# Three Newton steps instead of four in the reciprocal square root of a two-model transformer kernel

## The chip, the cores and the metric

The kernel runs on one core of one Trainium2 chip. The metric is the device time of one execution in microseconds (us), as the median of several runs; lower is better. Before the change three runs gave a median of 2302.99 us (2299.04 to 2307.05). TensorE (PE in the profile, with PEld for its weight loads) multiplies matrices, VectorE (DVE) and ScalarE (ACT) work elementwise, GpSimd (POOL) helps with elementwise work, and SyncE (SP) issues the DMAs.

## The reference, cut to what matters

Two small transformer blocks are computed one after the other on 512 tokens (and 256 context tokens) of width 1024. The first block has a linear recurrence layer (an RWKV-7 mixer with 16 heads, scanned forwards and backwards) and a differential attention layer; the second has two layers that mix causal, dilated and memory attention. The change touches only the normalisations, which stand in nearly every stage:

```python
def rms_norm(x, g, eps=RMS_EPS):
    xf = x.astype(jnp.float32)
    y = xf * lax.rsqrt(jnp.mean(xf * xf, axis=-1, keepdims=True) + eps)
    return (y * g.astype(jnp.float32)).astype(x.dtype)
...
    kk = heads(k * k_k)
    kk = kk * lax.rsqrt(jnp.sum(kk * kk, axis=-1, keepdims=True) + 1e-12)
...
    y = ((o - mean) * lax.rsqrt(var + GN_EPS)).reshape(B, T, RW_WIDTH) * gn_g + gn_b
```

## The kernel before

All large products are written as three TensorE products of a value split in two parts (high and low), so TensorE carries the bulk. The work falls into stages that follow each other in time, here with their place in the trace:

- 0 to 33 us, `startup` (L106): token blocks are loaded, normalised, turned with TensorE and modulated, while 1 MB weight pieces `ada_w` come in.
- 33 to 520 us, the input projections (`project`, L246) of the recurrence layer, with the preparation of the scan (`prep`, `products`, `invert`) woven in. `head_rsqrt` (L260) normalises the keys of each of 8 feature blocks, and of two memory blocks.
- 520 to 1115 us, the recurrence itself (`chain`) and its readouts (`readout`, L898 to L909), then the output projection of that layer.
- 1115 to 1600 us, the differential attention layer (`phase_4`): `Dense.heads` (L1276) makes normalised queries and keys, `attention` uses them. For each head pair, attention of one pair is interleaved with the projections of the next; the first pair's projections (`kqv(0)`) stand alone.
- 1600 to 2300 us, the two layers of the second block (`phase_5`), built alike from `Dense.heads`, `values`, `gates` and `attention`; each begins with a memory query projection (`mem(0)`) and ends with an output projection (`out_layer`), whose `Norm.rstd` (L1446 on) makes the next layer's norm.

The reciprocal square root is a helper, `rsqrt_dve` (L67 to L77). It makes a first guess from the bits of the value (L72) and then improves it in Newton steps of three VectorE instructions each (L74, L75, L76), every one of which reads the result of the one before. The tiles are small, 128 partitions by 1 to 24 numbers. It is called at eight places, 64 times in a run: `startup` L135 (3 times, tile `v`), `head_rsqrt` L272 (10, `hr_v`), `memory_norm` L416 (2, `m_v`), `readout` L899 and L906 (5, `vc`), `Dense.heads` L1300 (22, `hsv`), `Norm.rstd` L1452 (14, `nv`) and the end of a head in `phase_4`, L1607 (8, `ovv`). So L74, L75 and L76 run 256 times each.

The result is used right behind the last step: in `heads` by a multiplication on VectorE (L1303) that TensorE's transposes (L1359) wait for, in `phase_4` by L1608 before the transposes of L1611, in `readout` by a ScalarE copy (L873) before those of L876, in `startup` by L137 before those of L142, in `head_rsqrt` by a ScalarE copy (L274) before those of L280.

Each engine runs its instructions in the order of its own queue. That order is not the order of the Python code: the program is traced in an order that weaving loops set by credits (`weave`, `run_streams`) and priorities, and a planner then lays out each engine's queue by simulating a timeline in which each instruction has a modelled cost:

```python
    with tile.TileContext(nc, schedule_with_timeline_sim=True) as tc:
        run(tc, i, out)
```

So instructions of one Newton chain can stand between those of other work on VectorE's queue. One kind of such work is the weight split (L1071 and L1073): ScalarE rounds a raw weight tile `w_raw` to `w_hi`, and VectorE (90 times) or GpSimd (30 times) subtracts to get `w_lo`, which the projections' matmuls (L1092) read.

Of the kernel before, what the change touches and what calls it, by code (L numbers as in the profile page):

```python
# [66 lines left out]
def rsqrt_dve(E, pool, v, n):  # L67

    nc = E.nc
    y = pool.tile([128, n], FT, name="rq_y", bufs=2)  # L70
    t = pool.tile([128, n], FT, name="rq_t", bufs=2)
    nc.vector.tensor_scalar(y.bitcast(I32), v.bitcast(I32), -0.5, float(0x5F3759DF), OP.mult, OP.add)  # L72
    for _ in range(4):
        nc.vector.tensor_tensor(t, y, y, OP.mult)  # L74
        nc.vector.scalar_tensor_tensor(t, t, -0.5, v, OP.mult, OP.mult)  # L75
        nc.vector.scalar_tensor_tensor(y, t, 1.5, y, OP.add, OP.mult)  # L76
    return y  # L77
# [28 lines left out]
def startup(E, hh, hl):  # L106
# [3 lines left out]
    with tc.tile_pool(name="su", bufs=1, reuse_waits="tile") as pool, \  # L110
# [18 lines left out]
        for b0, nb in ((0, 2), (2, 2), (4, 2)):  # L129
            for tb in range(b0, b0 + nb):  # L130
                junk = pool.tile([128, 1024], FT, name="junk", bufs=1)
                A.activation(junk, xs[:, tb, :], AF.Square, accum_out=ss[:, tb:tb + 1])
            v = pool.tile([128, nb], FT, name="v", bufs=2)
            V.tensor_scalar(v, ss[:, b0:b0 + nb], 1.0 / 1024, 1e-6, OP.mult, OP.add)
            r = rsqrt_dve(E, pool, v, nb)  # L135
            for j in range(nb):
                V.tensor_scalar(xs[:, b0 + j, :], xs[:, b0 + j, :], r[:, j:j + 1], None, OP.mult)  # L137
            for kb in range(0, 8, 2):
                ps = pp.tile([128, 2, nb, 128], FT, name="tp", bufs=2)
                for k in range(2):  # L140
                    for j in range(nb):
                        P.transpose(ps[:, k, j, :], xs[:, b0 + j, (kb + k) * 128:(kb + k + 1) * 128], E.ident)  # L142
                (A.copy if kb % 4 else V.tensor_copy)(
                    xt[:, kb:kb + 2, b0 * 128:(b0 + nb) * 128].rearrange("p k (j t) -> p k j t", j=nb), ps)
# [61 lines left out]
class Scan:  # L206
# [53 lines left out]
    def head_rsqrt(self, x, n, scale, eps, use):  # L260

        E, nc = self.E, self.E.nc
        sq = self.s3("sq")
        nc.scalar.activation(sq[:, :n], x, AF.Square)
        ps = self.px()
        nb = n // 128
        for b in range(nb):
            nc.tensor.matmul(ps[:, 2 * b:2 * b + 2], sq[:, b * 128:(b + 1) * 128], self.ones2, start=True, stop=True)
        v = self.dp.tile([128, 12], FT, name="hr_v", bufs=1)
        nc.vector.tensor_scalar(v[:, :2 * nb], ps[:, :2 * nb], scale, eps, OP.mult, OP.add)  # L270
        yield 0
        r = rsqrt_dve(E, self.dp, v[:, :2 * nb], 2 * nb)  # L272
        rb = sq
        nc.scalar.copy(rb[:, :n].rearrange("p (b d) -> p b d", d=64), r.unsqueeze(2).to_broadcast([128, 2 * nb, 64]))  # L274
        yield 0
        for a in range(0, n, 384):
            m = min(384, n - a)
            ps = self.px()
            for o in range(0, m, 128):
                nc.tensor.transpose(ps[:, o:o + 128], rb[:, a + o:a + o + 128], E.ident)  # L280
            use(ps[:, :m], a, m)
            yield 0
# [123 lines left out]
    def memory_norm(self):  # L406

        E, nc = self.E, self.E.nc
        for b in range(2):
            m, u = (self.dp.tile([128, 8, 128], FT, name="ada_s", bufs=2) for _ in range(2))  # L410
            flat = lambda t: t.rearrange("p k t -> p (k t)")
            nc.sync.dma_start(flat(m), E.i["mem"][b * 128:(b + 1) * 128])
            ss, v = (self.dp.tile([128, 1], FT, name=n, bufs=1) for n in ("m_ss", "m_v"))
            nc.scalar.activation(flat(u), flat(m), AF.Square, accum_out=ss)
            nc.vector.tensor_scalar(v, ss, 1.0 / 1024, 1e-6, OP.mult, OP.add)
            r = rsqrt_dve(E, self.dp, v, 1)  # L416
            nc.vector.tensor_scalar(m, m, r, None, OP.mult)
            yield 0
            for k in (0, 4):
                ps = self.px()  # L420
                for kb in range(4):
                    nc.tensor.transpose(ps[:, kb * 128:(kb + 1) * 128], m[:, k + kb, :], E.ident)
                nc.scalar.copy(flat(u)[:, k * 128:k * 128 + 512], ps)
                yield 0
            nc.sync.dma_start(E.MT[:, :, b * 128:(b + 1) * 128], u)
# [1525 lines left out]
```

## Time and profile before

| what | value |
|---|---|
| median of three runs | 2302.99 us (2299.04 to 2307.05) |
| the profiled execution, its own time | 2302.14 us |
| its span, first to last instruction | 2300.3 us |
| granted TensorE clock, mean over the span | 0.935 |
| PE busy | 2093.5 us, 91% |
| DVE busy | 1574.1 us, 68%, 3952 instructions |
| ACT busy | 1167.7 us, 51% |
| POOL busy | 688.1 us, 30% |

The busy time of an engine is the sum of what its instructions took. A group line gives a source line, the engine, what was written from what, the count, the busy time and the mean length of one, and then the idle time just before these instructions with what ended it. The chain of waits goes back from the last instruction: at each step to what released it, or to the instruction ahead of it on its engine; it is one path, and its pieces are times on that path. A timeline row is a start, a length, the engine and the line, and in brackets the idle time before it.

### The profile page before, as it was taken

Reading aid. Unit: us, or ns where it says so; the run is one execution under the profiler, and the core shown is the slowest. Engines: PE = TensorE matmul, PEld = TensorE weight load, DVE = VectorE, ACT = ScalarE, POOL = GpSimd, SP = SyncE. Lnnn points to the kernel's source line nnn. Section 1 sums busy time; section 2 is a strip of 40 time slices with the busy share of each in tenths; the row PEclk is TensorE's granted clock in tenths of the full one; section 3 lists DMA queues with packets and bytes.
Section 4 is the critical chain, followed back from the end, with each engine's and each line's share of the span. In section 5 each row is a group of like instructions: output and inputs, shape, how many; then the busy total and the mean of one; then the engine's idle time right before and its main releaser. Section 6 shows DMA issues by size and latency. Waiting matters only on the chain.

```text
span 2300.3 us, 49070 instructions
## 1 busy us (share of the span) xinstructions
PE 2093.5 (91%) x18914; PEld 1861.9 (81%) x18920; DVE 1574.1 (68%) x3952; ACT 1167.7 (51%) x2636; POOL 688.1 (30%) x993
## 2 busy tenths in 40 slices
PE   7999999987998988888979999997899999999989
PEld 3998899975777766666979889887888988888878
DVE  5468968987278887734676786854686674767673
ACT  4455456563255453433346465563465564556652
POOL 0133523534036363322312232312222232033221
PEclk9999999985999788877999999998999999999999
DMA  7467456347644333154121111142222223322132
GB/s 248 137 188 235 158 172 220 114 144 230 204 115 139 105 98 115 34 163 159 56 70 49 60 42 65 42 124 79 97 83 68 80 74 108 113 65 65 60 104 81
DMA packets 189592, 262.55 MB, mean 114 GB/s; under 512 B 16048, under 2 KB 136368, under 8 KB 189232
## 3 DMA queue, kind: packets, MB, share of 16 engines
q1 hardware_dynamic: 189360, 259.43, 35.6%
q8 instruction: 149, 2.44, 0.4%
q14 instruction: 83, 0.68, 0.1%
HBM read 196.72 MB, written 62.65 MB: 113 GB/s over the span
## 4 chain that ended last, share of the span: by engine, by line
PE 45%; DVE 13%; DMA 5%; ACT 4%; issue 3%; POOL 2%; SPq 0%; ACTq 0%; DVEq 0%; POOLq 0%
PE ps_pj L1092 25%; PE ps_s L1389 3%; DMA w_raw<-in_wd_dram 2%; PE ps_t L1781 2%; PE ps_t L1599 2%; PE ps_b L579 1%; PE ps_s L1092 1%; PE ps_t L1767 1%; PE ps_m L85 1%; DMA w_raw<-att 1%; DVE hx L1303 1%; DVE w_lo L1073 1%; PE ps_t L1359 1%; PE ps_t L1588 1%; DVE al L556 1%
## 5 line engine op out<-in xcount | busy, mean ns | idle before, releaser
L1092 PE MATMUL ps_pj<-w_hi,act 128*128 128x256 f32 x3264 | 646.3, 292 | 22.0 <-ACT act L1472 4.8
L1092 PEld LDWEIGHTS ps_pj<-w_hi,act 128*128 128x128 f32 x3264 | 530.6, 196 | 36.0 <-ACT act L1472 7.0
L1092 PE MATMUL ps_pj<-w_lo,act 128*128 128x256 f32 x1632 | 472.7, 290 | 0.0
L1092 PEld LDWEIGHTS ps_pj<-w_lo,act 128*128 128x128 f32 x1632 | 320.0, 196 | 1.2 <-issue 0.9
L246 PE MATMUL ps_pj<-h,b_hi 128*128 128x384 f32 (+1 forms) x1216 | 316.4, 341 | 2.7 <-ACT gh L352 1.5
L246 PEld LDWEIGHTS ps_pj<-h,b_hi 128*128 128x128 f32 x1216 | 220.1, 193 | 8.6 <-ACT gh L352 2.7
L246 PE MATMUL ps_pj<-h,b_lo 128*128 128x384 f32 (+1 forms) x608 | 207.3, 342 | 0.4 <-DVE b_lo L190 0.4
L1071 ACT CAST w_hi<-w_raw 128x1024 fp32r<-128x1024 f32 x120 | 121.2, 1050 | 63.0 <-DMA w_raw<-in_wd_dram 33.0
L1073 DVE TENSOR_TENSOR w_lo<-w_raw,w_hi 128x1024 fp32r<-128x1024 f32 x90 | 121.7, 1358 | 40.9 <-ACT w_hi L1071 40.1
L1073 POOL TENSOR_TENSOR w_lo<-w_raw,w_hi 128x1024 fp32r<-128x1024 f32 x30 | 72.5, 2415 | 252.5 <-ACT w_hi L1071 252.5
L1092 PE MATMUL ps_pj<-act,w_hi 128*128 128x256 f32 x768 | 145.7, 285 | 0.0
L1757 POOL TENSOR_SCALAR p<-p,r 128x128 f32<-128x128 f32 (+2 forms) x64 | 71.6, 1119 | 236.5 <-DVE r L1751 151.1
L579 PE MATMUL ps_b<-al,bk 64*128 64x128 f32 x768 | 123.8, 303 | 11.0 <-DVE rbk L587 9.9
L579 PEld LDWEIGHTS ps_b<-al,bk 64*128 64x128 f32 x768 | 102.6, 202 | 32.8 <-issue 20.1
L1092 PEld LDWEIGHTS ps_pj<-act,w_hi 128*128 128x128 f32 x768 | 120.7, 191 | 0.4 <-issue 0.2
L246 PEld LDWEIGHTS ps_pj<-h,b_lo 128*128 128x128 f32 x608 | 117.2, 193 | 3.6 <-issue 1.3
L547 POOL TENSOR_TENSOR s<-bk,src 64x256 f32<-64x256 f32 x96 | 77.5, 807 | 124.0 <-DVE bk L544 111.5
L1092 PE MATMUL ps_pj<-act,w_lo 128*128 128x256 f32 x384 | 109.7, 286 | 0.0
L1315 POOL TENSOR_TENSOR hx<-hx,ctab 128x256 f32<-128x256 f32 x80 | 67.1, 857 | 135.9 <-DVE ht L1313 119.7
L1578 POOL TENSOR_TENSOR p<-p 128x768 f32<-128x768 f32 x32 | 60.6, 1894 | 154.3 <-ACT p L1577 81.5
L1389 PE MATMUL ps_s<-k_s,q_hi 128*128 128x256 f32 (+2 forms) x256 | 88.5, 355 | 9.8 <-ACT p L1748 5.9
L189 ACT CAST b_hi<-b_raw 128x512 fp32r<-128x512 f32 x84 | 52.1, 622 | 71.1 <-PE ps_pj L246 56.6
(325 smaller groups left out, 4943.9 us busy)
## 6 DMA issues: line engine op xcount, KB each, us to landing
w_raw<-in_wd_dram SPq DMA_DIRECT2D x120, 512.0 KB, 4.2
b_raw<-in_blocks_dram SPq DMA_DIRECT2D x84, 256.0 KB, 3.1
src<-streams SPq DMA_DIRECT2D x48, 384.0 KB, 3.8
ada_s<-in_ada_w_dram SPq DMA_DIRECT2D x24, 512.0 KB, 4.4
vs<-streams SPq DMA_DIRECT2D x48, 256.0 KB, 3.2
ada_w<-in_ada_w_dram SPq DMA_DIRECT2D x8, 1024.0 KB, 11.0
lr<-lora SPq DMA_DIRECT2D x96, 64.0 KB, 3.1
streams<-k SPq DMA_DIRECT2D x32, 192.0 KB, 2.8
```

The source lines that it names most:

```text
L189: nc.scalar.copy(hi, raw)
L246: E.nc.tensor.matmul(ps[gi][:, :m], w[:, kb % 4, :], h[:, kb, :], start=(n[gi] == 1), stop=(n[gi] == 24))
L547: G.tensor_tensor(v3(rev(s))[a:a + 64], ut[a:a + 64, 1 if a == 0 else 0], v3(rev(r))[a:a + 64], OP.mult)
L579: P.matmul(pb[:, c, :], bk[q:e, c].rearrange("p s t -> p (s t)"), al[q:e, c, h:3:2 - h, :], start=True, stop=True, tile_position=(q, 0))
L1071: nc.scalar.copy(hi[:, a:a + 4], raw)
L1073: e.tensor_tensor(lo[:, a:a + 4], raw, hi[:, a:a + 4], OP.subtract)
L1092: E.nc.tensor.matmul(ps, a(kb), b(kb), start=(k == 0), stop=(k == 23))
L1315: G.tensor_tensor(w4(x), w4(x), cb, OP.mult)
L1389: P.matmul(ps, q[i][:, 2 * j + h, c], k[h][:, j, a:a + n], start=(i == 0), stop=(stop and i == 1))
L1578: G.tensor_tensor(ps_[0], ps_[0], ps_[1], OP.add)
L1599: P.matmul(ps[:, :128], pt[:, kb, :], v[:, kb, h * 128:(h + 1) * 128], start=(kb == 0), stop=(kb == 5))
L1757: G.tensor_scalar(t, t, r[:, h:h + 1], None, OP.mult)
```

## The change

The loop in `rsqrt_dve` runs three times instead of four; nothing else is edited.

```diff
@@ -70,7 +70,7 @@
     y = pool.tile([128, n], FT, name="rq_y", bufs=2)
     t = pool.tile([128, n], FT, name="rq_t", bufs=2)
     nc.vector.tensor_scalar(y.bitcast(I32), v.bitcast(I32), -0.5, float(0x5F3759DF), OP.mult, OP.add)
-    for _ in range(4):
+    for _ in range(3):
         nc.vector.tensor_tensor(t, y, y, OP.mult)
         nc.vector.scalar_tensor_tensor(t, t, -0.5, v, OP.mult, OP.mult)
         nc.vector.scalar_tensor_tensor(y, t, 1.5, y, OP.add, OP.mult)
```

## Rows read from the trace of the kernel before

**Rows 1.** The page's busy time, share of the span and instructions of each engine.

```profile
PE 2093.5 (91%) x18914; PEld 1861.9 (81%) x18920; DVE 1574.1 (68%) x3952; ACT 1167.7 (51%) x2636; POOL 688.1 (30%) x993
```

**Rows 2.** Busy time in windows: window, length, engines (counts), clock, DMA share, GB/s.

```profile
33.00:520.00 487.00, 473.09 (x3265) 427.51 (x3263) 368.47 (x788) 261.58 (x545) 163.08 (x290) 0.97 0.54 171
660.00:1050.00 390.00, 341.94 (x4883) 272.51 (x4882) 285.48 (x661) 177.61 (x368) 163.90 (x336) 0.86 0.38 112
1180.00:1600.00 420.00, 385.49 (x2979) 365.06 (x2978) 287.78 (x733) 232.88 (x506) 115.95 (x83) 0.96 0.20 64
2000.00:2230.00 230.00, 216.26 (x1749) 196.72 (x1749) 166.24 (x446) 139.80 (x356) 68.04 (x61) 0.99 0.24 75
```

**Rows 3.** VectorE's busy time in L74 to L76 alone, over the whole span.

```profile
0.00:2301.00 2301.00, 172.16 (x768) 0.93 0.36 114
```

**Rows 4.** Timeline of one call at the end of the readouts, last step.

```profile
1053.85 0.17 DVE L76 SCALAR_TENSOR_TENSOR rq_y<-rq_t,rq_y 128x16 f32<-128x16 f32 x1
1054.06 0.17 DVE L74 TENSOR_TENSOR rq_t<-rq_y 128x16 f32<-128x16 f32 x1
1054.26 0.17 DVE L75 SCALAR_TENSOR_TENSOR rq_t<-rq_t,vc 128x16 f32<-128x16 f32 x1
1054.47 0.18 DVE L76 SCALAR_TENSOR_TENSOR rq_y<-rq_t,rq_y 128x16 f32<-128x16 f32 x1
1054.68 1.14 ACT L873 COPY rb<-rq_y 128x512 f32<-128x512 f32 x2 [4.61 <-DVE rq_y L76]
```

**Rows 5.** The chain of waits: first, three long and last piece of L74 to L76.

```profile
1052.17 0.18 DVE rq_t L74
...
1125.06 0.74 DVE rq_y L76
...
1378.19 2.34 DVE rq_y L76
...
2185.30 2.05 DVE rq_t L75
...
2191.39 0.19 DVE rq_y L76
```

**Rows 6.** TensorE's waits: line waited for, us in total, times, longest.

```profile
PE ps_t L1359 <- DVE hx L1309: 11.5, 3, 5.0
...
PE ps_t L1611 <- DVE o L1608: 7.7, 3, 4.3
...
PE ps_m L876 <- ACT rb L873: 3.6, 1, 3.6
...
PE ps_x L280 <- ACT sq L274: 2.5, 1, 2.5
```

**Rows 7.** Timeline of the startup, first call and what follows it.

```profile
15.17 0.16 DVE L76 SCALAR_TENSOR_TENSOR rq_y<-rq_t,rq_y 128x2 f32<-128x2 f32 x1
...
15.39 6.08 PE L85 MATMUL ada_ps<-ada_w,cs 128*2 128x256 f32 x16 [15.39 <-DVE rq_y L76]
...
21.40 1.09 PE L142 MATMUL tp<-ident,x_in 128*128 128x128 f32 x8
```

**Rows 8.** Timeline of a GpSimd weight split beside the end of a call.

```profile
1378.12 2.39 POOL L1073 TENSOR_TENSOR w_lo<-w_raw,w_hi 128x1024 fp32r<-128x1024 f32 x1 [1.17 <-ACT w_hi L1071]
1378.19 2.33 DVE L76 SCALAR_TENSOR_TENSOR rq_y<-rq_t,rq_y 128x4 f32<-128x4 f32 x1
...
1380.56 0.69 DVE L1608 TENSOR_TENSOR o<-o,rq_y 128x512 f32<-128x512 f32 x1
```

**Rows 9.** Timeline of the first call in the attention layer.

```profile
1178.96 0.18 DVE L72 TENSOR_SCALAR rq_y<-hsv 128x24 int32<-128x24 int32 x1
1179.22 1.23 DVE L1073 TENSOR_TENSOR w_lo<-w_raw,w_hi 128x1024 fp32r<-128x1024 f32 x1
1180.37 0.18 DVE L74 TENSOR_TENSOR rq_t<-rq_y 128x24 f32<-128x24 f32 x1
1180.46 1.22 DVE L1073 TENSOR_TENSOR w_lo<-w_raw,w_hi 128x1024 fp32r<-128x1024 f32 x1
1181.60 0.18 DVE L75 SCALAR_TENSOR_TENSOR rq_t<-rq_t,hsv 128x24 f32<-128x24 f32 x1
```

## The prediction, made before the change was run

> **What bounds the kernel now.** I read the page's busy times first. TensorE is busy 91% of the span, VectorE, where the change acts, 68% [rows 1]. Then the same by stage, to see whether some stage has VectorE in front: between 33 and 520 us TensorE is busy 473.1 of 487 us, in the attention layers 385.5 of 420 and 216.3 of 230, against 287.8 and 166.2 for VectorE; the recurrence from 660 to 1050 us has the two nearest together, 341.9 and 285.5 of 390 [rows 2]. So VectorE is nowhere the engine that is always busy. What a shorter Newton chain is worth must be read from the places where TensorE stands still for its result, and from the chain of waits, which shows the same by pieces of time.
>
> **What goes.** The loop is unrolled when the program is built: 64 calls lose three instructions each, 192 of VectorE's 3952. The four steps take 172.16 us in 768 instructions [rows 3], so a quarter, 43.0 us of VectorE's busy time, goes. Nothing is added, no DMA is moved, and no wait is made: the consumer reads the result of the third step instead of the fourth. Where a call runs undisturbed, its last three instructions start 0.21 us apart, from 1054.06 to 1054.68 [rows 4], so each result is ready 0.62 us sooner. Over 64 calls that is 64 x 0.62 = 39.7 us of latency, the other reading of the same 43.0.
>
> **How much of it lies on the path.** The chain of waits holds 153 pieces of L74 to L76, from 1052.17 to 2191.39 us [rows 5], 33.7 us together. Eleven of them are long, 0.43 to 2.34 us, 13.6 us in sum (three stand in rows 5). With these eleven counted as 0.2 us each, as the ordinary ones are, the sum is 33.7 - 13.6 + 11 x 0.2 = 22.3 us. One step in four goes: 22.3 / 4 = 5.6 us. Issue gaps of 0.02 us follow the pieces, 2.5 us in all; a quarter is 0.6. That makes **6.2 us**.
>
> The long pieces I pass on rather than count. At 1378.19 the last instruction of a call, on 4 numbers per partition, takes 2.33 us; a GpSimd subtraction ran from 1378.12 to 1380.51, and the two end within 0.01 us of each other [rows 8]. What holds VectorE there is GpSimd's instruction, so with the fourth step gone the next reader of two tiles in that place would be held instead, unless it got ahead. If they did shrink by a quarter as well, 33.7 / 4 + 0.6 = 9.0 us would come off. The Trainium skill says the same of these two engines (SBUF — State Buffer, "SBUF: two separate sides"): they share a port pair that whoever starts first keeps for its whole instruction. By that rule the sum stays at 6.2; without it, at 9.0. The trace agrees in this one place, 2.33 beside 2.39 us [rows 8].
>
> The bound from below: with the queue order kept, the chain overstates, because when it gets shorter a path beside it takes over. The surest part is where TensorE shows itself idle behind such a result: three stops before L1359, three before L1611 and one before L876 [rows 6], where nothing of another head pair stands beside the call. Seven times 0.62 us is 4.3 us. I take 6.2, nearer to 4.3 than 9.0 is, and keep both ends. Below 4.3, down to 0, is a case of its own.
>
> **What is hidden.** The chain doesn't reach back before 637 us, so the 15 calls of the startup and the projections are judged apart. In the startup the first result comes at 15.33 us, but TensorE then works 6.08 us on `ada_ps` before the transposes that use it start at 21.40 [rows 7]: that is cover enough for 0.6 us. The third startup call may show; I give it 0, bounded by 0.6. In the projections TensorE idles 13.9 of 487 us altogether [rows 2], and waits once, 2.5 us, behind `head_rsqrt` [rows 6]; I cost it at 0, bounded by 0.6. The cover is the projections' own matmuls; without them each call would show its 0.62.
>
> The sum is 2302.1 - 6.2 = 2295.9 us for the profiled execution (span 2300.3 and 1.8 around it). Its own time stands 0.85 below the median of the three runs, so against the median it is 2303.0 - 6.2 = **2296.8 us**, 0.27% less. About 0.3%, 6.9 us, is what a measurement of this kernel can tell from no change.
>
> **Rival 1, hidden.** VectorE is idle 32% of the time and TensorE has queued work of other heads; a result 0.6 us sooner then only makes VectorE idle longer. For it: TensorE's waits of rows 6 are only 25.3 of its 207 idle us. Against it: in the seven stops nothing else stands beside the call. Gain 0 to 4 us: about 2301. The Trainium skill would go further (Perfetto Trace Analysis, "Identifying the Most-Contended Engine"): improve the engine with the highest occupancy first, which by rows 1 is not VectorE, and the sum by it would be 0. The trace bears it out over most of the span, not in those seven stops.
>
> **Rival 2, more than the chain.** VectorE serves one queue. In the attention layers it is 69 to 72% busy [rows 2], and 43.0 us less of its work also brings forward what stands behind each call. For it: pieces of the calls stand between instructions of other streams on the chain. The gain is bounded by those 43.0 us (2260); TensorE's idle time of 34.5 and 13.7 us in the two attention windows [rows 2] lets a part of it come home, some 10 to 18 us, so about 2290.
>
> **Rival 3, the planner lays the queues anew: slower.** Each queue's order comes from a simulated timeline with modelled costs, so 192 fewer instructions flip near ties everywhere behind the first. The place where a flip costs most: in the first call of the attention layer two weight splits of 1.23 us stand inside the Newton chain, between L72 and the first L75 [rows 9], while TensorE's longest stop of 5.0 us runs [rows 6]. There are 90 such splits on VectorE and 44 calls (22, 14 and 8) in the dense layers. Each further split laid in front of a result that TensorE waits for costs 1.23 us. It decides the sign by more than 6.9 us from (6.2 + 6.9) / 1.23 = 10.7, so 11 of the 44 calls, on. With 13 it is 2303.0 - 6.2 + 16.0 = 2312.8 us. For it: nothing holds the order in place, and two such splits already stand there. Against it: flips go either way, and they would have to fall on one side eleven times. That the edit doesn't do what it says is excluded by the code: every step is three instructions issued by a Python loop.
>
> **The numbers.** The forecast, 4.3 to 9.0 us off (2294 to 2299), has 0.42. Rival 1 has 0.22, rival 2 0.16, rival 3 0.20. Faster by over 0.3% is rival 2 and the 0.24 of the forecast beyond 6.9 us: 0.40. Within 0.3% is the forecast's other 0.18 and rival 1: 0.40. Slower by over 0.3% is rival 3: 0.20. The forecast's own range is 2294 to 2299; the range over the cases goes from 2285, which leaves out the far half of rival 2's reach to 2260 (about 0.05), to 2313, which takes in rival 3 up to 13 flips and leaves out the rest (about 0.10).
>
> **What the profile of the changed kernel should show.** VectorE with 3760 instructions and some 1531 us busy; L74 to L76 with 576 instructions in about 129 us; TensorE's waits for L1309 down from 11.5 to some 9.6 us, for L1608 from 7.7 to 5.8, for L873 from 3.6 to 3.0. If those waits shrink and the time does not, rival 1 holds. If weight splits stand in other places on VectorE's queue and the waits behind them have grown, rival 3. I would be wrong in the main if the time moved by over 9 us either way: then order, not latency, made it.

## The result and the profile after

The changed kernel took 2314.38 us (median of 20 runs, 2303.43 to 2320.85), against 2301.32 us for the kernel before in the 20 runs beside it (2294.33 to 2311.49): a ratio of **1.0058, 95% interval 1.0042 to 1.0074**, so 13 us slower, by 0.58%. A second measurement of it (*changed_again*, below) gave 1.0024 (0.9997 to 1.0052). Weighted by their intervals the two make 1.0050, some 11 us. Either way it lies on the other side from the forecast of 2296.8 us, though the second measurement alone can't be told from no change.

The instructions went as the diff says. On the page of the changed kernel the engines' busy times answer to [rows 1], and the window of L74 to L76 alone to [rows 3]:

```profile
PE 2104.4 (91%) x18914; PEld 1873.3 (81%) x18920; DVE 1537.7 (66%) x3760; ACT 1168.9 (50%) x2636; POOL 683.9 (30%) x993
```

```profile
0.00:2330.00 2330.00, 133.96 (x576) 0.93 0.35 113
```

VectorE has its 192 instructions less and 36.4 us less of busy time, and the span still grew from 2300.3 to 2316.6 us. TensorE, with the same 18914 matmuls, is busy 10.9 us longer, and stands idle 2316.6 - 2104.4 = 212.2 us instead of 206.8 (2300.3 - 2093.5). Where does that lie? I cut each span in three at matmuls that every version has: the first and the last start of the recurrence's first product (L733, 768 matmuls). Columns as in [rows 2]; the rows are of before, then of the changed kernel, then of its second profile.

```profile
0.00:545.49 545.49, 505.98 (x3401) 447.08 (x3401) 401.69 (x898) 288.39 (x591) 171.95 (x312) 0.95 0.57 183
545.49:1041.56 496.07, 435.15 (x6518) 347.37 (x6518) 340.08 (x786) 211.95 (x453) 186.68 (x404) 0.85 0.42 127
1041.56:2300.30 1258.74, 1152.41 (x9002) 1067.46 (x9004) 832.31 (x2269) 667.32 (x1592) 329.42 (x278) 0.96 0.24 79
```

```profile
0.00:538.94 538.94, 507.78 (x3400) 450.10 (x3401) 393.43 (x843) 285.40 (x590) 165.11 (x304) 0.95 0.57 184
538.94:1056.34 517.40, 446.78 (x6519) 357.32 (x6520) 337.34 (x784) 216.01 (x457) 187.40 (x412) 0.84 0.41 124
1056.34:2316.60 1260.26, 1149.86 (x9000) 1065.90 (x9002) 806.97 (x2133) 667.47 (x1590) 331.33 (x278) 0.96 0.24 79
```

```profile
535.65:1044.49 508.84, 446.64 (x6519) 357.36 (x6520) 337.53 (x784) 215.22 (x457) 186.37 (x412) 0.84 0.42 126
1044.49:2299.10 1254.61, 1142.79 (x9000) 1059.33 (x9002) 807.67 (x2133) 667.37 (x1590) 330.10 (x278) 0.97 0.24 79
```

Read the second column (length) and the third (PE busy, with its count). The changed kernel reaches the recurrence 6.6 us sooner, loses 21.3 us in it (12.8 in the second profile), and behind it stands about where before stood, though 136 VectorE instructions are gone there. The recurrence's loss is in part idle time, and in both profiles some 11.5 us more busy time for the same number of matmuls. So the first profile's loss needed two questions, which the experiments put: is it the step that was taken out, or the order in which the planner laid the queues without it; and how much of it is TensorE's clock, which scatters by itself?

### The profile page after: what moved, and what is told of

Read it like the earlier page. It is cut to its first block, busy times and chain, and to the rows that moved or that the text cites. A ratio compares the mean times of both kernels' runs of the same rounds, so it can differ in the third digit from the quotient of the medians.

```text
span 2316.6 us, 48876 instructions
## 1 busy us (share of the span) xinstructions
PE 2104.4 (91%) x18914; PEld 1873.3 (81%) x18920; DVE 1537.7 (66%) x3760; ACT 1168.9 (50%) x2636; POOL 683.9 (30%) x993
## 4 chain that ended last, share of the span: by engine, by line
PE 41%; DVE 16%; DMA 5%; ACT 4%; issue 4%; POOL 1%; SPq 0%; ACTq 0%; DVEq 0%; POOLq 0%
PE ps_pj L1092 22%; PE ps_s L1389 2%; DMA w_raw<-in_wd_dram 2%; PE ps_t L1781 2%; PE ps_t L1599 1%; DVE w_lo L1073 1%; PE ps_b L579 1%; PE ps_s L1092 1%; PE ps_t L1767 1%; DVE hx L1303 1%; ACT w_hi L1071 1%; PE ps_m L85 1%; DVE hx L1316 1%; DVE ht L1313 1%; DVE ut L657 1%
## 5 line engine op out<-in xcount | busy, mean ns | idle before, releaser
L1092 PEld LDWEIGHTS ps_pj<-w_hi,act 128*128 128x128 f32 x3264 | 531.9, 196 | 41.3 <-ACT ht L1294 11.5
L1757 POOL TENSOR_SCALAR p<-p,r 128x128 f32<-128x128 f32 (+2 forms) x64 | 72.3, 1130 | 246.5 <-DVE r L1751 194.6
L579 PE MATMUL ps_b<-al,bk 64*128 64x128 f32 x768 | 129.7, 314 | 14.2 <-DVE rbk L587 12.0
L579 PEld LDWEIGHTS ps_b<-al,bk 64*128 64x128 f32 x768 | 108.2, 214 | 35.6 <-issue 23.0
## 6 DMA issues: line engine op xcount, KB each, us to landing
ada_w<-in_ada_w_dram SPq DMA_DIRECT2D x8, 1024.0 KB, 11.7
```

The costliest lines, as they stand in the source:

```text
L579: P.matmul(pb[:, c, :], bk[q:e, c].rearrange("p s t -> p (s t)"), al[q:e, c, h:3:2 - h, :], start=True, stop=True, tile_position=(q, 0))
L1092: E.nc.tensor.matmul(ps, a(kb), b(kb), start=(k == 0), stop=(k == 23))
L1757: G.tensor_scalar(t, t, r[:, h:h + 1], None, OP.mult)
```

## The experiments

The eight places call the helper 64 times, numbered k in the order of the program; calls 0 to 19 are those of startup, projections and recurrence, 20 to 63 those of the dense layers. Each kernel here is the one before with this edit, and a choice of PLAN and REAL. PLAN(k) steps are given to the planner, and the order that it lays out for each engine is read; REAL(k) steps are then built. Where the two differ, the real program's instructions are tied, engine by engine, to the plan's order, with no wait added; the instructions of a step more stand straight behind the third step, those of a step less are simply missing. Their lines stand 6 or 8 further down (L733 is L739).

```diff
-    for _ in range(4):
+    k, E.calls = E.calls, E.calls + 1
+    for s in range(E.steps(k)):
...
+    info = mybir.DependencyInfo(mybir.DependencyClass.NoSync, mybir.DependencyReason.DATA)
+    for q in queues.values():
+        last = None
+        todo = [here[n] for n in q if n in here]
...
+            if last is not None:
+                tc.add_manual_dep(x, last.name, info, reason="order of the plan")
+            last = x
```

`q` is one engine's queue in the plan, and `here` finds the real program's instruction for each of its names. All ratios are to the kernel before in runs beside them; where one line below sets both PLAN and REAL, or names several kernels, it stands for a line for each.

**old_order_3**: three steps, in before's order on every queue.

```diff
+PLAN = lambda k: 4
+REAL = lambda k: 3
```

> Three steps, with every engine's queue held in the order of the kernel before (the instructions of the fourth step are taken out, nothing else moves). If the new order of the queues made the loss: the time of before less what the prediction's chain gives, 2301.3 - 6.2 = 2295.1 us, between 4.3 and 9.0 us off, ratio 0.996 to 0.998. If the shorter calls themselves cost time (results that come sooner start other work that collides): slower as the change was, about 2314 us, ratio 1.006. If the latency is hidden: 2301 us, ratio 1.000.

**new_order_4**: four steps, in the changed kernel's order.

```diff
+PLAN = lambda k: 3
+REAL = lambda k: 4
```

> Four steps, with every engine's queue held in the order of the changed kernel, the three instructions of the fourth step put straight behind the third. If the new order made the loss: the time of the changed kernel and 6.2 us more, about 2320.6 us, ratio 1.008 (1.006 if the latency is hidden). If the shorter calls themselves cost time: back to about 2301 us, ratio 1.000.

Measured: old_order_3 2281.28 us, ratio **0.9931 (0.9900 to 0.9962)**; new_order_4 2335.89 us, **1.0174 (1.0145 to 1.0203)**. Both went the way expected if the order makes the loss (0.996 to 0.998 and 1.008), and both further. With the changed kernel and the one before that is a square of two step counts and two orders. At before's order the step is worth 16 us in the right direction; at the new order some 27 us (1.0174 to 1.0058). The new order costs 1.3% at three steps (0.9% by the second measurement of the changed kernel) and 1.7% at four. The sign of the result is the order's.

The traces bear out that the order was held. Leaving out L74 to L76, VectorE runs 3184 instructions in each kernel: in old_order_3 they stand in before's sequence without exception, in new_order_4 in the changed kernel's, while the changed kernel has 1456 of them at their place of before. Nor do the ties add instructions: the profile of old_order_again (below) holds 48878, which is before's 49070 less 192. A kernel with four steps tied to its own order, which would show directly what the ties cost, was not run; a cost of the ties of some 3 us would make the two worths of the step alike at an equal clock (9 and 15 us, below) and change no sign.

**three_early** and **three_late**: the planner free, three steps in the first 20 calls or in the last 44.

```diff
+PLAN = REAL = lambda k: 3 if k < 20 else 4   # three_early
+PLAN = REAL = lambda k: 4 if k < 20 else 3   # three_late
```

> Three steps in the 20 calls ahead of the attention layers (startup, keys, memory, readouts), four in the 44 after; the planner is free. If order is the cause, and most of all that of the recurrence: the recurrence ends 10 to 15 us later than before, as in the changed kernel, and what the later layers then do is open, 2303 to 2318 us. If the loss goes with the number of steps taken out: 20/64 of 13 us, about 2305 us.

> Four steps in the 20 calls ahead of the attention layers, three in the 44 after; the planner is free, so all queues are as before up to the first of these. If order is the cause: the recurrence loses nothing, and the attention layers gain or lose by chance, 2290 to 2310 us. If the loss goes with the number of steps taken out: 44/64 of 13 us, about 2310 us, all of it behind 1115 us.

Measured: three_early 2310.39 us, 1.0058 (1.0034 to 1.0082); three_late 2296.09 us, 0.9998 (0.9972 to 1.0025). The stage lengths in the table below say why: three_early loses in the recurrence (516.2 us) and nothing behind it; three_late keeps the recurrence (490.9) and loses behind it, where it has 1256.3 us against 1243.6 in old_order_3. There are two losses, and each comes with the shortened calls of its own part of the program.

**first_call_3, changed_again, old_order_again**: one step less in the first startup call only; the changed kernel and old_order_3 once more.

```diff
+PLAN = REAL = lambda k: 3 if k == 0 else 4   # first_call_3
+PLAN = REAL = lambda k: 3                    # changed_again
+PLAN = lambda k: 4; REAL = lambda k: 3       # old_order_again
```

> The planner free, three steps in the first call of the startup alone, four elsewhere: three instructions less, and every queue keeps before's order. The prediction costs this call at 0: ratio 0.999 to 1.001, and TensorE's busy time within 5 us of before's 2093.5. If the busy time differs by 10 us or more at an unchanged order, the granted clock scatters from run to run and the busy part of the other differences (10.9 us in the changed kernel) can't be put down to the order.

> The changed kernel once more, same order on every queue. If the order decides: ratio again 1.004 to 1.008, the recurrence again 515 to 520 us long between the first and the last matmul of its first product, TensorE busy 2100 to 2109 us. If the granted clock scatters by itself: the recurrence 500 us or less, or busy under 2095.

> Before's order held, three steps, once more. If the 16 us of old_order_3 belong to it: ratio 0.991 to 0.996, TensorE busy 2073 to 2083 us, TensorE's idle time 197 to 201 us. If 16.2 of its 24 us were scatter of the granted clock: busy near 2093 in this profile, idle again 197 to 201 us, and the ratio nearer to 0.997.

Measured: first_call_3 1.0007 (0.9982 to 1.0032), TensorE busy 2095.7 us; changed_again 1.0024 (0.9997 to 1.0052), recurrence 508.8 us, busy 2094.9; old_order_again 0.9939 (0.9917 to 0.9962), busy 2094.5 and idle 195.8 us. These are part misses, and useful ones. The ratio of old_order_3 came again, its busy time of 2077.3 us did not: 16 to 17 us of a single profile's busy time can be the scatter of the granted clock at one and the same order, so neither a span nor a busy time of one profile is to be read finer than 10 us. TensorE's **idle time** is steadier, though not everywhere: 199.0 and 195.8 us at before's order with three steps, 206.8 and 207.9 with four (207.9 with one call shortened), but 212.2 and 204.2 in the two profiles of the changed kernel. Those two differ in the recurrence (70.6 and 62.2 us); behind it they agree (110.4 and 111.8), as the pairs at before's order do (106.3 and 104.3 with four steps, 97.7 and 98.2 with three).

That scatter can be taken out in good part. In 123 runs of the kernel before, the span falls by 15.5 us for each 0.01 of mean granted clock (0.926 to 0.944; correlation -0.90). Each run shifted by that slope to a clock of 0.934 gives the last column here; the stage lengths are those of the profiled run, cut as above.

| kernel | to recurrence | recurrence | rest | ratio | mean clock | span at clock 0.934 |
|---|---|---|---|---|---|---|
| before | 545.5 | 496.1 | 1258.7 | 1 | 0.934 | 2299.8 |
| first_call_3 | 545.0 | 501.8 | 1256.8 | 1.0007 | 0.935 | 2301.3 |
| changed kernel | 538.9 | 517.4 | 1260.2 | 1.0058 | 0.934 | 2311.2 |
| changed_again | 535.6 | 508.8 | 1254.7 | 1.0024 | 0.937 | 2309.5 |
| old_order_3 | 541.0 | 491.7 | 1243.6 | 0.9931 | 0.941 | 2290.3 |
| old_order_again | 544.3 | 500.4 | 1245.6 | 0.9939 | 0.938 | 2291.0 |
| new_order_4 | 543.2 | 514.0 | 1271.9 | 1.0174 | 0.929 | 2325.3 |
| three_early | 537.1 | 516.2 | 1259.9 | 1.0058 | 0.932 | 2305.3 |
| three_late | 545.2 | 490.9 | 1256.3 | 0.9998 | 0.937 | 2300.1 |
| old_order_2 | 538.9 | 493.6 | 1242.8 | 0.9899 | 0.939 | 2286.7 |
| old_order_0 | 539.0 | 495.1 | 1234.5 | 0.9877 | 0.938 | 2280.3 |
| free_2 | 526.7 | 520.2 | 1242.7 | 0.9954 | 0.938 | 2296.2 |
| one_call_3 | 545.8 | 491.3 | 1265.1 | 0.9972 | 0.939 | 2303.1 |
| hold_first | 544.4 | 479.8 | 1256.6 | 0.9913 | 0.946 | 2297.9 |
| hold_recurrence | 545.5 | 493.2 | 1249.7 | 0.9960 | 0.940 | 2299.8 |
| hold_scan | 543.0 | 497.6 | 1246.5 | 0.9938 | 0.940 | 2296.3 |
| hold_dense | 540.0 | 513.0 | 1242.4 | 0.9978 | 0.935 | 2296.8 |
| hold_filler | 538.4 | 505.2 | 1251.1 | 0.9963 | 0.941 | 2300.3 |
| hold_ends | 540.2 | 478.2 | 1247.7 | 0.9886 | 0.943 | 2286.5 |

At an equal clock the step is worth 9 us at before's order and 15 at the new one, and the new order costs 20 us at three steps and 25 at four. The clock itself is not the same either from order to order, which widens the measured ratios: 0.938 to 0.941 at before's order with three steps, 0.929 for new_order_4, 0.946 for hold_first. So the last column also takes out what an order or a step does to the clock: the ratios tell what an edit is worth in all, this column what it is worth beside the clock.

**old_order_2** and **old_order_0**: before's order, two steps and no step. They leave out one and three more Newton steps; old_order_0 leaves out the whole refinement.

```diff
+PLAN = lambda k: 4
+REAL = lambda k: 2   # old_order_0: 0
```

> Before's order held on every queue, two Newton steps in every call (two steps' instructions, 384, are left out, so the roots are rounder than fp32). Theory A (at a held order a step is worth what old_order_3 measured, 16 us, because the same dependent chain is on the path again): ratio about 0.986, 32 us off. Theory B (the chain of waits, 6.2 us a step, and old_order_3 was helped by something else): about 0.990, 16 + 6 = 22 us off. If a path beside it has taken over (diminishing): 0.991 to 0.993.

> Before's order held on every queue, no Newton step at all (768 instructions left out; the first guess from the bits is used as it is). Theory A: 4 x 16 = 64 us off, ratio 0.972. Theory B: 16 + 3 x 6.2 = 35 us off, 0.985. Diminishing: between 0.985 and 0.993.

Measured: 0.9899 (0.9868 to 0.9931) and 0.9877 (0.9849 to 0.9905). At clock 0.934 the first step is worth 9, the second 4, the last two 6 together; TensorE's idle time goes 206.8, 199.0, 192.8, 187.3 us. By the ratios the second step is worth 7 us, so 16 us for every step is refuted, and the last two are worth 5 us together. The chain's 6.2 lies between the two readings of the second step; the last two, at some 3 us each, show diminishing returns. With intervals of 0.3% each, these single steps are near the limit of what the times can tell. The waits show the plain part of it. TensorE's waits that answer to [rows 6], first with old_order_3, then with old_order_0:

```profile
PE ps_t L1365 <- DVE hx L1315: 9.9, 3, 4.4
PE ps_t L1617 <- DVE o L1614: 3.7, 1, 3.7
PE ps_m L882 <- ACT rb L879: 3.0, 1, 3.0
```

```profile
PE ps_t L1365 <- DVE hx L1315: 8.1, 3, 3.6
PE ps_t L1617 <- DVE o L1614: 1.9, 1, 1.9
PE ps_m L882 <- ACT rb L879: 1.1, 1, 1.1
```

The single stop behind the readout goes 3.6, 3.0, then 2.4 at two steps and 1.1 at none: 0.62 us a step, as [rows 4] have it. The longest stop of L1614 goes 4.3, 3.7, 3.1, 1.9. Two shorter stops of that line were gone with the first step: with that the seven stops give 22.8 - 16.6 = 6.2 us in all instead of 4.3. How many of the shorter stops go is partly luck, however: old_order_again, with the same queues, keeps one of them (L1614 5.0 us in two stops) and gives 4.9, and first_call_3, at before's order with all those calls unchanged, has 6.6 us for that line instead of 7.7.

**free_2** and **one_call_3**: the planner free, two steps everywhere, or three in a single call of the projections.

```diff
+PLAN = REAL = lambda k: 2                     # free_2
+PLAN = REAL = lambda k: 3 if k == 10 else 4   # one_call_3
```

> The planner free, two Newton steps in every call (384 instructions left out). If fewer steps mean less time whatever the order, this is faster than the changed kernel by a step at least: 1.006 - 0.007 = 0.999 or less. If the order decides (the loss of the changed kernel is one draw among many), the ratio is anywhere in 0.975 to 1.01 and differs from old_order_2 by several tenths of a per cent; I expect 0.995.

> The planner free, three steps in one single call (the sixth call of head_rsqrt, in the projections), four in the 63 others: 3 instructions and 0.6 us of latency less. Theory A for the order (near ties flip anywhere behind the first difference, and which way is chance): the queues differ in well over a thousand rows, and the time differs from before's by more than 0.1% either way, range 0.995 to 1.012. Rival (the loss comes from something that only many shortened calls bring): 0.9995 to 1.0005.

Measured: free_2 0.9954 (0.9928 to 0.9980), so 0.55% behind old_order_2, which runs the same instructions; one_call_3 0.9972 (0.9953 to 0.9991). Three instructions less in one call re-laid the queues from there on (the first startup call, by contrast, moved nothing). one_call_3 has the recurrence 5 us shorter and the rest 6 us longer than before in its profile, and a higher clock. At an equal clock it is 3 us slower than before. Its 0.28% for 0.6 us of latency fits an order drawn anew and not the rival's 0.9995 to 1.0005. free_2 by itself doesn't decide: 0.9954 is what I expected of a draw, and it is also under 0.999, as "fewer steps, less time" asks.

**hold_first, hold_recurrence, hold_scan, hold_dense**: three steps; only one part's instructions are tied among themselves to before's order (0 = startup and projections, 1 = recurrence, 2 = dense layers), the planner places the rest.

```diff
+PLAN = lambda k: 4
+REAL = lambda k: 3
+HOLD = (0,)   # hold_recurrence (1,), hold_scan (0, 1), hold_dense (2,)
-        todo = [here[n] for n in q if n in here]
+        todo = [here[n] for n in q if n in here and part[n] in HOLD]
```

> Three steps everywhere; the instructions of startup and projections stand among themselves in before's order on every queue, all others are placed by the planner. Theory A (the loss in the recurrence comes from how the recurrence's own instructions are laid out): the recurrence still loses, ratio 1.000 to 1.006. Rival (the loss is brought in by the order of the projections and the readiness it leaves): 0.993 to 0.998, as the recurrence then keeps before's pace.

> Three steps everywhere; only the instructions of the recurrence stage stand among themselves in before's order, all others are placed by the planner. Theory A: the 18 to 21 us lost between the first and the last matmul of L733 do not appear; with the loss at the layer boundaries of about 8 to 13 us left, the ratio is 0.996 to 1.000. Rival (order of the projections): 1.002 to 1.006.

> Three steps everywhere; projections and recurrence in before's order, the dense layers behind them are placed by the planner. Theory A: no loss in the recurrence, that of the dense layers' new order remains in part: 0.994 to 0.999. If the dense layers' order costs nothing by itself, 0.993 as in old_order_3.

> Three steps everywhere; only the dense layers' instructions (attention layers and second block) stand among themselves in before's order, projections and recurrence are placed by the planner. Theory A (the loss sits in the recurrence first): the recurrence loses its 18 to 21 us, the layer boundaries lose nothing, 1.000 to 1.004. If the dense layers' order is the larger part of the loss: under 0.998.

Measured: hold_first 0.9913 (0.9886 to 0.9939), hold_recurrence 0.9960 (0.9937 to 0.9983), hold_scan 0.9938 (0.9913 to 0.9962), hold_dense 0.9978 (0.9951 to 1.0005). hold_recurrence and hold_scan came where my theory had them or beside it. hold_dense did so by its stages alone (513.0 us in the recurrence, 1242.4 behind it); its ratio stands where I had put the other reading, under 0.998, and its interval takes in both. hold_first, faster than either of its ranges, refutes the theory's first half: the recurrence's own order need not be held. Behind projections in before's order the planner's recurrence is among the shortest, 479.8 us (and 478.2 in hold_ends, below); behind projections that the planner laid with three steps or fewer in their calls it takes 509 to 520. So what is laid earlier bears on how what follows comes out. Much of hold_first's gain goes with its higher clock: at 0.934 it would be 2 us ahead of before.

**hold_ends**: projections and dense layers in before's order, the recurrence free.

```diff
+HOLD = (0, 2)
```

> Three steps; projections and dense layers in before's order, the recurrence laid out by the planner, which did best so in hold_first. If the parts add up: hold_first's recurrence (480 us) and hold_dense's layer boundaries (8 to 12 us less than in the changed kernel) together, about 10 us under hold_first: ratio 0.986 to 0.990. If the recurrence's layout depends on what stands behind it: 0.991 to 0.997.

Measured: 2274.70 us, ratio **0.9886 (0.9855 to 0.9918)**, 26 us less than before: the parts add up as expected (0.986 to 0.990), and this version beats both kernels. Its lead over old_order_3 is 4 us at an equal clock, and by the ratios their intervals overlap. Its two later stages:

```profile
540.24:1018.48 478.24, 427.11 (x6520) 339.28 (x6520) 334.32 (x774) 212.51 (x455) 182.38 (x404) 0.88 0.44 132
1018.48:2266.20 1247.72, 1147.97 (x9000) 1064.57 (x9002) 808.00 (x2133) 666.00 (x1590) 329.69 (x278) 0.96 0.24 80
```

**hold_filler**: the changed kernel, but on TensorE's queue the matmuls of L85, L526 and L733 keep before's sequence among each other. I had read in the two profiles of the changed kernel that the first 12 steps of the recurrence take some 107 us instead of 96, with 24 matmuls of this filler work (16 of L85, 8 of L526) moved from the first six steps to the next six. Windows of six steps each, for before, the changed kernel, and hold_filler:

```profile
545.49:606.11 60.62, 51.03 (x897) 0.77 0.64 203
606.11:641.81 35.70, 33.03 (x618) 1.00 0.59 183
```

```profile
538.94:598.70 59.76, 46.34 (x873) 0.78 0.66 202
598.70:645.52 46.82, 40.19 (x643) 0.93 0.53 162
```

```profile
538.40:609.28 70.88, 55.36 (x896) 0.72 0.60 188
609.28:645.26 35.98, 33.30 (x618) 1.00 0.56 177
```

```diff
+HOLD = (1,)
...
-        todo = [here[n] for n in q if n in here and part[n] in HOLD]
+        todo = [here[n] for n in q if n in here and part[n] in HOLD and n in KEEP]
```

`KEEP` holds the names of the matmuls of L85, L526 and L733.

> The changed kernel (three steps, planner free) but for one thing: on TensorE's queue, in the recurrence stage, the matmuls of the lora (L526), of the modulation columns (L85) and of the recurrence's first product (L733) stand among each other in before's sequence; no other instruction is held. If the place of this filler work costs the recurrence its time: from the first matmul of the recurrence to the one 12 steps on 95 to 99 us (as with before's order; 106.6 and 107.1 in the two profiles of the changed kernel), and the ratio 0.998 to 1.003. If other instructions of the new order (inversion, readout) make the loss: 105 us or more there, and the ratio 1.003 to 1.007.

Measured: 0.9963 (0.9938 to 0.9988). The reading is refuted: the second window is back at 36 us, the first grew by 11, and step 12 comes at 645.3 us as in the changed kernel. What the pairs of windows show instead lies in their starts: the changed kernel reaches the recurrence 6.6 us sooner and gets to step 12 no sooner than before does (645.5 and 641.8 us). The kernel as a whole did become faster than the changed one, but which of the instructions that moved with the filler did that stays open.

## Why the prediction was wrong

**The sum.** Its parts held better than its total. L74 to L76 have 576 instructions left and 134.0 us (129 forecast; 128.97 in old_order_3). In the changed kernel L1309's stops went from 11.5 to 9.9 us (9.6 forecast) and L1608's from 7.7 to 5.5 (5.8), but L873's, forecast to fall from 3.6 to 3.0, rose to 7.2, because a new stop of 4.2 us stands beside the old one. The changed kernel's waits that answer to [rows 6]:

```profile
PE ps_t L1359 <- DVE hx L1309: 9.9, 4, 4.4
PE ps_m L876 <- ACT rb L873: 7.2, 2, 4.2
PE ps_t L1611 <- DVE o L1608: 5.5, 3, 3.8
```

The whole, 6.2 us with bounds of 4.3 and 9.0, measured at before's order is 16 us (14 in old_order_again). At an equal clock it is 9, at the upper bound; the rest goes with the granted clock, which rose from 0.934 to 0.938 or more, and for that I had no term. So at a kept order the chain did not overstate, as I had feared in the bound from below. TensorE's idle time fell by 7.8 and 11.0 us in the two profiles, mostly behind the recurrence.

**The long pieces** did pass on, in part. In old_order_3 L74 to L76 lost 172.16 - 128.97 = 43.2 us of busy time, but VectorE as a whole only 1574.1 - 1540.6 = 33.5, about 192 ordinary instructions of 0.18 us [rows 4]: some 10 us of held time turned up on other instructions. In the changed kernel, where VectorE has 1537.7 us and not 1531, most of the difference is still in L74 to L76 (134.0 for 129). The Trainium skill's rule (SBUF — State Buffer, "SBUF: two separate sides"), by which VectorE and GpSimd take turns at a shared port pair, agrees with [rows 8] and with the held time as far as it goes; no run tested whether all of the held time is of that kind.

**The step that failed** stands in one clause of the prediction: "with the queue order kept". The sum put the new order at nothing. Nothing keeps the order, and its price, 20 us at an equal clock, is more than twice the gain. I knew of it as rival 3, gave it 0.20, and asked for eleven flips on one side. That was the wrong count: one kind of place need not flip many times, because what stands behind the first difference is laid anew. In one_call_3, with 3 instructions less in a call at 349 us, VectorE's sequence leaves before's at 356 us, and 561 of 3184 instructions stand in another place.

**Rival 3** was right in kind and in sign, and wrong in place. Weight splits did not move in front of the calls: inside Newton chains there are 39 of them instead of 36, and the first call of the attention layer has the same two as in [rows 9]. The loss lies in two other places.

In the **dense layers** three waits of TensorE grew that have no Newton step in them: projections for the squares of the head ahead (L1294, ScalarE, which reads the PSUM tile), and transposes for the rescaled scores (L1757, GpSimd) and for an output (L1397, VectorE). Waits from the end of the recurrence on, in us, times and longest: before, changed kernel, old_order_3.

```profile
PE ps_t L1767 <- POOL p L1757: 6.1, 10, 1.9
PE ps_pj L1092 <- ACT ht L1294: 3.3, 5, 1.0
PE ps_t L1767 <- DVE y L1397: 2.3, 6, 0.5
```

```profile
PE ps_t L1767 <- POOL p L1757: 10.7, 12, 2.6
PE ps_pj L1092 <- ACT ht L1294: 9.7, 8, 2.6
PE ps_t L1767 <- DVE y L1397: 4.5, 8, 1.3
```

```profile
PE ps_t L1773 <- POOL p L1763: 5.9, 9, 1.9
PE ps_pj L1098 <- ACT ht L1300: 3.2, 4, 1.8
PE ps_t L1773 <- DVE y L1403: 2.6, 7, 0.5
```

The three sum to 11.7 us before and in old_order_3, and to 24.9 in the changed kernel, 13.2 more. TensorE's idle time behind the recurrence is 1243.6 - 1145.9 = 97.8 us and 1260.3 - 1149.9 = 110.4: 12.6 more. So these waits are as large as that loss; others rose and fell around them (transposes' waits for L1737, VectorE, fell from 5.7 us to 0.9). It repeats: changed_again has 11.2, 9.7 and 5.4; three_late 8.1, 10.0 and 4.0; three_early, whose dense calls keep four steps, 5.9, 3.1 and 2.3; and hold_dense 5.9, 2.1 and 2.5. But the three waits don't set the time alone: in hold_scan, whose dense layers the planner laid with three steps, they sum to 21.7 us, and TensorE's idle time there is 102.3, only 4.6 more than in old_order_3.

In the **recurrence** the loss is broader: 509 to 517 us in the changed kernel's two profiles against 492 to 500 at before's order with three steps, part idle, part clock. Which moves make all of it stays open. One place shows how a stop and the clock hang together, and also what a planner does to a Newton chain. In the third readout call of the changed kernel, VectorE's timeline:

```profile
969.13 0.18 DVE L74 TENSOR_TENSOR rq_t<-rq_y 128x24 f32<-128x24 f32 x1
...
969.82 0.17 DVE L74 TENSOR_TENSOR rq_t<-rq_y 128x24 f32<-128x24 f32 x1
970.01 2.04 DVE L661 STREAM_TRANSPOSE ut<-ut 128x1024 f32<-128x1024 f32 x1
971.97 1.19 DVE L663 STREAM_TRANSPOSE ut<-ut 128x1024 f32<-128x1024 f32 x1
973.09 0.13 DVE L75 SCALAR_TENSOR_TENSOR rq_t<-rq_t,vc 128x24 f32<-128x24 f32 x1
973.25 2.06 DVE L676 COPY lb<-ut 32x1024 f32<-32x1024 f32 x2
975.24 0.16 DVE L76 SCALAR_TENSOR_TENSOR rq_y<-rq_t,rq_y 128x24 f32<-128x24 f32 x1
...
975.88 0.18 DVE L76 SCALAR_TENSOR_TENSOR rq_y<-rq_t,rq_y 128x24 f32<-128x24 f32 x1
```

Work of the triangular inversion stands inside the second step, and the call takes 7.2 us from its guess to its end; the same call of before, with a step more, took 3.9. TensorE stood behind it, yet not for the chain itself. The result was ready at 976.06, and ScalarE's copy L873, for which TensorE waits, starts only at 977.05, with no idle time before it: ahead of it on ScalarE's queue stand two copies of the inversion (L676), which had waited for VectorE's L663. So what ended last is the inversion's work on both queues; a Newton result ready sooner would not have shortened this stop. ScalarE's timeline, then TensorE's:

```profile
973.19 3.84 ACT L676 COPY lb<-ut 32x1024 f32<-32x1024 f32 x2 [3.95 <-DVE ut L663]
977.05 1.14 ACT L873 COPY rb<-rq_y 128x512 f32<-128x512 f32 x2
```

```profile
977.72 1.11 PE L876 MATMUL ps_m<-ident,rb 128*128 128x128 f32 x4 [4.16 <-ACT rb L873]
```

Windows of 4 us (length, PE busy with its count, granted clock, DMA share, GB/s):

```profile
966.00:970.00 4.00, 3.87 (x78) 1.00 0.20 53
970.00:974.00 4.00, 2.06 (x80) 1.00 0.08 23
974.00:978.00 4.00, 0.28 (x2) 0.64 0.00 0
978.00:982.00 4.00, 3.59 (x60) 0.50 0.00 0
982.00:986.00 4.00, 4.00 (x91) 0.50 0.02 6
986.00:990.00 4.00, 4.00 (x93) 0.50 0.02 4
990.00:994.00 4.00, 4.00 (x88) 0.50 0.00 0
```

The clock is 1.00 (2.4 GHz) until the stop and 0.50 (1.2 GHz) behind it, and stays there to 994 us, with TensorE busy 15.6 of the 16 us from 978 on. In this place the stop of 4.2 us thus costs more than itself. It stands at 4.2 us in changed_again and three_early as well, and nowhere in the recurrence of before, old_order_3 or hold_ends. It doesn't make the recurrence's loss by itself, since before's kernel is at 0.50 in that stretch too, behind other stops; hold_ends passes it at 1.00. Rival 3 had priced a flip at 1.23 us, the length of what moves, with no term for the clock behind a stop.

**Rival 1** is refuted at before's order, where the step shows. **Rival 2** (10 to 18 us from work brought forward) is what the ratio of old_order_3 looks like, but at an equal clock it is 9, so its mechanism isn't shown.

**Startup and projections at 0** held, as far as the traces tell; the ratio of first_call_3, 1.0007, is too wide (0.9982 to 1.0032, some 6 us either way) to show 0.6 us. [rows 7] put the wait of the first `ada_ps` matmul down to the Newton chain; in first_call_3 the chain ends 0.64 us sooner, at 14.69 us, and that matmul starts at 15.33 all the same (15.39 before), where the profile has it wait for its weights:

```profile
15.33 5.04 PE L91 MATMUL ada_ps<-ada_w,cs 128*2 128x256 f32 x16 [15.33 <-DMA ada_w<-in_ada_w_dram]
```

Up to the recurrence TensorE is idle 39.5 and 41.2 us with four steps in all calls or all but one, and 40.6 and 38.8 at before's order with three.

The rule of the Trainium skill that I weighed with rival 1 (Perfetto Trace Analysis, "Identifying the Most-Contended Engine"), to optimise the engine with the highest occupancy first, I had read as setting the sum at 0; the runs at a held order gave 14 to 16 us for an engine that is busy 68%.

The last sentence of the prediction named its own test, a move of over 9 us either way, and "order, not latency" as the reading of it. That was the right reading.

## What to carry to other kernels

Where a planner lays out the queues, an edit of any size is two edits: what it says, and a new order of much that follows. Measure the first by building the new instructions in the old order, and price the second as a spread: here orders of the same instructions, with three steps, lay between 0.989 and 1.006 of the time before, while the edit itself was worth 0.007. If the old order is the better one, keep it, and try it part by part: the projections and the dense layers held and the recurrence left free took 0.9886.

## What the runs showed of the hardware that was not expected

The mean granted clock of one and the same program ran from 0.926 to 0.944 over 123 runs, and each 0.01 of it went with 15.5 us, more than the 9 us that the edit is worth at an equal clock. TensorE's busy time moved with it (2077.3 and 2094.5 us for the same queues), its idle time less (199.0 and 195.8 there; behind the recurrence 110.4 and 111.8 in the changed kernel, though 70.6 and 62.2 within it). Where a few microseconds decide, idle time and waits of one stage are therefore the steadier thing to compare between two profiles, and the median over many runs is the only time to trust.
